# Adaptive-norm weights accumulated for pairs of feature blocks, and rotary tables made with the input tiles: one change to a decoder-layer kernel on one core

## The chip, the core and the metric

The kernel runs on one core of a Trainium2 chip. The metric is device time in microseconds (us) of one execution; before the change the median of three runs is 790.29 us (788.85 to 792.57). Inputs and output are float32 in HBM. The engines are named as in the profile: PE is the matmul engine (PEld its weight loads), DVE the vector engine, ACT the scalar engine, POOL GpSimd, SP the engine that issues nearly all DMAs.

## The reference, cut to what matters

One layer, 1024 tokens, 1024 features. The part that the change touches is the first: an adaptive norm, followed by the input projection.

```python
mod = jax.nn.silu(c) @ ada_w[l] + ada_b[l]          # (1, 1024) @ (1024, 3072)
shift, scl, gate = jnp.split(mod, 3, axis=-1)
h = rms_norm(x, norm_g[l]) * (1.0 + scl[:, None, :]) + shift[:, None, :]
proj = h @ w_in[l]                                  # split into 13 parts
...
ang = pos.astype(jnp.float32)[..., None] * inv      # rotary: cos(ang), sin(ang)
```

After it come two groups of attention heads, their gates, the output projection, a residual and a last norm. None of that is changed.

## The kernel before

**The stage.** `h` is needed with features on partitions, so `x` (8 tiles of 128 tokens) is scaled by its row norm, turned on PE (`xT`) and stored as `xnT`, 8 blocks of 128 features by 1024 tokens. Block k becomes `h` by one multiply and add per feature: `ab[:, 0, k]` (from `scl`) and `ab[:, 1, k]` (from `shift`) are one column each. ACT writes `hh[k]` (rounded to the matmul type) and `hf` (full float32), one after the other (`h_high`, L307 to L310); DVE makes `hl[k] = hf - hh[k]` (`h_low`, L312). Two parts of the projection are then accumulated over the eight blocks: `kcT` (`mm_kc`, 512-column products: four for hh with the weights' high part `whia`, four with their low part `wloa`, four for hl) and `ks` (`mm_ks`, 256 columns, as many). The low parts of the weights are made by POOL (`w_split`, L263) from DMA'd pieces that hold two blocks each.

**The modulation columns.** The weights for block k are 8 pieces (one per 128 inputs of `c`) of 128 x (2 x 128), loaded by `ad_load` as two tiles `ad` with four DMAs. In `mod_acc` the pieces 0 to 5 go to DVE: one `TENSOR_SCALAR` and five `SCALAR_TENSOR_TENSOR` of 256 columns build up `acc` (L288, L290). Pieces 6 and 7 go to PE as four one-column products (L284). `mod_mm` sums `acc` over partitions by two products with a column of ones (L297), and `mod_cols` makes the columns of `ab` in three small DVE instructions (L302 to L305). Block 0 is done by 16 one-column products on PE alone, spread over the last input tiles.

**The order.** The whole stage is inside one `manual_schedule` over all five engines, so each engine's order is that of the Python calls. First a loop over the input tiles (L463), whose step s has `x_stat(s)` (squares on ACT, `rv` on DVE), `x_turn(s - 1)` and `x_put(s - 2)`; `ACC0` adds parts of `mod_acc`. Then a software pipeline (L490) whose step s_ works on several blocks at once: weights for block s_ and s_ - 1 accumulated piece by piece between each other (`skew`), columns and `h_high` of block s_ - 1, and on PE the products with hh of block s_ - 2 and those with hl of block s_ - 3. The rotary tables are DVE work on 384 columns (`trig`, L394): their positions are loaded late (L459) and turned on PE in steps 3 to 5, and the tables stand in steps 7 and 8. The SP queue is in order: a load whose buffer is still in use holds the ones behind it. `x` and `ad` share 8 buffers of the tag `big`.

Of the kernel before, what the change touches and what calls it, by code (L numbers as in the profile page):

```python
# [107 lines left out]
def hybrid_block(ctx, tc, x, c, positions, ada_w, ada_b, norm_g, w_in, cmp_pos, cmp_k_w1, cmp_k_w2,  # L108
# [157 lines left out]
    def ad_load(k):  # L266
        ads[k] = []
        for q in range(AD_CUT):
            n = KD // AD_CUT
            ad = sp.tile([P, 1024], F32, name=f"ad{k}_{q}", tag="big", bufs=8).rearrange("p (k j n) -> p k j n", k=n, j=2)  # L270
# [21 lines left out]
    def mod_mm(k):  # L292
        if k in MOD_PE:
            return
        acc = accs.pop(k)
        for j in range(2):
            nc.tensor.matmul(pas[k][:, j:j + 1], acc[:, j, :], ones_pp[:, 0:1], start=False, stop=True,  # L297
                             skip_group_check=True)

    def mod_cols(k):  # L300
        pa = pas.pop(k)
        nc.vector.scalar_tensor_tensor(sums[:, k:k + 1], pa[:, 0:1], 1.0, cols[:, 16 + k:17 + k],  # L302
                                       op0=ALU.add, op1=ALU.add)
        nc.vector.tensor_tensor(ab[:, 0, k:k + 1], sums[:, k:k + 1], cols[:, 32 + k:33 + k], op=ALU.mult)
        nc.vector.tensor_tensor(ab[:, 1, k:k + 1], pa[:, 1:2], cols[:, 8 + k:9 + k], op=ALU.add)  # L305
# [141 lines left out]
    with tc.manual_schedule(engines={mybir.EngineType[e] for e in ENGS0}):  # L447
        nc.sync.dma_start(rows[0:8], c.rearrange("o (k p) -> (o k) p", p=P))
        x_load(0)
        small_loads()  # L450
        for t in range(1, X_AD):
# [7 lines left out]
        pos_loads()  # L459
# [3 lines left out]
        for s_ in range(NT + 2):  # L463
# [14 lines left out]
        def skew(k, i0, i1):  # L478
            for i in range(i0, i1):
                if k < KD:  # L480
                    mod_acc(k, 4 + i, 5 + i)
                if k + 1 < KD:
                    mod_acc(k + 1, i, i + 1)

# [4 lines left out]
        mod_acc(1, 2, 4)  # L489
        for s_ in range(1, KD + 3):  # L490
            if s_ + 1 < KD:
                ad_load(s_ + 1)
            if s_ % 2 == 1 and s_ // 2 + 1 < KD // 2:
                kc_raw(s_ // 2 + 1)
                ks_raw(s_ // 2 + 1)
            if 1 < s_ < KD:
                (kc_split if s_ % 2 else ks_split)(s_ // 2)
            if MOD_FIRST <= s_ <= KD:
                mod_mm(s_ - 1)
# [1096 lines left out]
```

## Time and profile before

| what | value |
|---|---|
| median of 3 runs | 790.29 us (788.85 to 792.57) |
| the profiled execution | 788.64 us, span 786.9 us |
| PE busy | 739.3 us, 94% of the span |
| DVE, ACT, POOL busy | 583.6, 396.3, 228.0 us |
| mean granted PE clock | 0.970 of full |
| the stage that the change touches | span start to about 82 us |

The profile is of one execution. Its time beside its span leaves 1.7 us that lie outside the first and last instruction. Times in the rows further below count from the span's start; busy shares are averages over stages with different limits, so what a change in the first 82 us is worth is read from those 82 us. A clock of 1.00 is PE's upper level (2.4 GHz), 0.50 the lower (1.2 GHz). A float32 product shows as two PE records, so four one-column products are "x8".

### The profile page before, as it was taken

To read this page: it belongs to the slowest core of one execution; us is meant where nothing else is said; L and a number is where in the kernel's file an instruction comes from. 1 tells how busy PE (TensorE), PEld (TensorE's weight loads), DVE (VectorE), ACT (ScalarE), POOL (GpSimd) and SP (SyncE) were. 2 spreads that over 40 slices of the span, in tenths; PEclk is the share of its full clock that TensorE was granted. 3 is DMA by queue.
4 is the path that set the end of the run, shared out by engine and by line. 5 is a ranking of instruction groups with operands and counts; after the bars stand their busy time and mean duration, and the time that the engine had idled before them with its cause. 6 is when DMAs were issued, how large, how long until landed. Compare 5 with 4: busy or idle time off the path is not lost.

```text
span 786.9 us, 17257 instructions
## 1 busy us (share of the span) xinstructions
PE 739.3 (94%) x6464; PEld 653.9 (83%) x6464; DVE 583.6 (74%) x1549; ACT 396.3 (50%) x697; POOL 228.0 (29%) x287
## 2 busy tenths in 40 slices
PE   4999999999999999997899999999988989999996
PEld 3988998989999999995677887777877777888885
DVE  3688745587688788888898889987888878654433
ACT  5354534133122331217899977987556566632212
POOL 3334433154231143504443312110200040154322
PEclk9599999999999999999999999999999979999999
DMA  8961423242531121103311123013010140435431
GB/s 307 262 197 49 127 55 108 61 121 80 162 95 48 44 52 47 36 31 97 93 47 44 43 56 82 22 57 80 10 28 16 52 151 29 151 131 185 144 113 54
DMA packets 60513, 70.18 MB, mean 89 GB/s; under 512 B 5957, under 2 KB 46728, under 8 KB 60430
## 3 DMA queue, kind: packets, MB, share of 16 engines
q1 hardware_dynamic: 55646, 64.62, 27.8%
q10 hardware_dynamic: 4784, 4.47, 1.7%
q8 instruction: 51, 0.84, 0.4%
q14 instruction: 32, 0.26, 0.1%
HBM read 48.33 MB, written 11.53 MB: 76 GB/s over the span
## 4 chain that ended last, share of the span: by engine, by line
PE 76%; DVE 9%; issue 4%; ACT 4%; DMA 4%; POOL 2%; SPq 1%; POOLq 0%; DVEq 0%; ACTq 0%
PE pj L589 24%; PE out L1528 11%; PE o L937 5%; PE pm L841 4%; PE s L994 3%; PE s L995 3%; PE kcT L321 2%; PE mo L937 2%; PE hid L642 2%; PE kq L1180 2%; PE ms L1301 2%; DVE L L1010 2%; PE ms L1302 2%; PE ms L1303 2%; PE mm L1256 2%
## 5 line engine op out<-in xcount | busy, mean ns | idle before, releaser
L589 PE MATMUL pj<-whi,hh 128*128 128x288 f32 (+2 forms) x544 | 161.4, 297 | 0.0
L589 PE MATMUL pj<-wlo,hh 128*128 128x288 f32 (+2 forms) x544 | 158.6, 292 | 0.0
L589 PE MATMUL pj<-whi,hl 128*128 128x288 f32 (+2 forms) x544 | 157.6, 290 | 0.0
L589 PEld LDWEIGHTS pj<-wlo,hh 128*128 128x128 f32 x544 | 102.5, 189 | 1.4
L589 PEld LDWEIGHTS pj<-whi,hh 128*128 128x128 f32 x544 | 102.5, 189 | 0.4
L589 PEld LDWEIGHTS pj<-whi,hl 128*128 128x128 f32 x544 | 102.2, 188 | 0.0
L1010 DVE TENSOR_TENSOR L<-E,H 128x1024 f16<-128x1024 f32 x74 | 92.0, 1243 | 13.1 <-ACT H L1005 11.4
L799 DVE CUSTOM_DVE_ANT_0 junk<-pm,maskw 128x256 bf16<-128x256 f32 (+3 forms) x160 | 77.7, 486 | 16.4 <-PE pm L841 4.4
L1004 ACT ACTIVATE E<-s 128x1024 f32<-128x1024 f32 x74 | 76.4, 1032 | 19.8 <-PE s L995 12.2
L937 PEld LDWEIGHTS <-H 128*128 128x128 f16 x1184 | 57.2, 97 | 30.2 <-issue 17.5
L968 POOL TENSOR_TENSOR mixn<-mixn,tmp 128x256 f32<-128x256 f32 x32 | 44.8, 1400 | 108.7 <-DVE tmp L967 101.9
L1005 ACT ACTIVATE H<-s 128x1024 f16<-128x1024 f32 x74 | 76.2, 1030 | 0.0
L841 PE MATMUL pm<-ka,qall 128*128 128x448 f32 (+5 forms) x208 | 67.2, 323 | 0.2 <-DVE mp L796 0.2
L937 PE MATMUL o<-v,H 128*128 128x65 f16 (+1 forms) x1056 | 60.0, 195 | 4.6 <-DVE mixn L964 4.6
L211 POOL TENSOR_TENSOR wlo<-wraw,whi 128x288 fp32r<-128x288 f32 (+2 forms) x64 | 51.7, 832 | 31.6 <-ACT whi L210 29.3
L994 PE MATMUL s<-qa,ka 128*128 128x512 f32 x132 | 57.9, 439 | 2.9 <-ACT H L1005 2.5
L937 PE MATMUL o<-v,L 128*128 128x65 f16 x528 | 56.7, 193 | 0.0
L937 PEld LDWEIGHTS <-L 128*128 128x128 f16 x592 | 55.7, 100 | 0.0
L708 ACT ACTIVATE zt<-pj 128x288 f32<-128x288 f32 (+1 forms) x32 | 12.2, 384 | 74.3 <-PE pj L589 62.6
L1314 ACT ACTIVATE lat<-ms 128x1024 f32<-128x1024 f32 (+2 forms) x40 | 32.6, 815 | 31.1 <-PE ms L1303 14.9
L1316 DVE TENSOR_TENSOR mL<-lat,mH 128x1024 f16<-128x1024 f32 (+2 forms) x40 | 39.0, 988 | 9.7 <-ACT mH L1315 9.5
L995 PE MATMUL s<-qall,kb_early 128*128 128x512 f32 x108 | 43.4, 401 | 0.0
(384 smaller groups left out, 1892.1 us busy)
## 6 DMA issues: line engine op xcount, KB each, us to landing
ad<-in_ada_w_dram SPq DMA_DIRECT2D x32, 256.0 KB
wraw<-in_w_in_dram SPq DMA_DIRECT2D x20, 288.0 KB
x<-in_x_dram SPq DMA_DIRECT2D x8, 512.0 KB
gw<-in_ada_w_dram SPq DMA_DIRECT2D x32, 128.0 KB
qa<-qall SPq DMA_DIRECT2D x32, 128.0 KB
wor<-in_w_out_dram SPq DMA_DIRECT2D x16, 256.0 KB
xr<-in_x_dram SPq DMA_DIRECT2D x8, 512.0 KB
out_dram<-y SPq DMA_DIRECT2D x7, 512.0 KB
```

The lines of the kernel that those rows point to most:

```text
L211: split.tensor_tensor(wlo[:, :width], raw[:, j, :width], f32(whi[:, :width]), op=ALU.subtract)
L589: nc.tensor.matmul(pt[:, :width], a[k][:, ts], b[:, :width], start=(n == 0), stop=(n == 23))
L799: nc.vector.tensor_tensor_reduce(out=junk[:, :w], in0=scores, in1=mask, scale=1.0, scalar=2.0 * NEG, op0=ALU.add, op1=ALU.max, accum_out=dst)
L841: nc.tensor.matmul(bank[:, :total_w], lhs, keys, start=True, stop=True)
L937: nc.tensor.matmul(po[:, c0:c0 + hi - lo], a[:n, qs], v[:, lo:hi], start=start and j == 0, stop=stop and j == 2, skip_group_check=True)
L968: nc.gpsimd.tensor_tensor(mv, mv, tmp, op=ALU.add)
L994: nc.tensor.matmul(dst, a, staged[u], start=True, stop=False)
L995: nc.tensor.matmul(dst, b, qc[u], start=False, stop=mk is None)
L1004: nc.scalar.activation(Et, pS, AF.Exp, scale=SC_NSA)
L1005: nc.scalar.activation(ph, pS, AF.Exp, scale=SC_NSA)
L1010: nc.vector.tensor_tensor(pl, Et, ph, op=ALU.subtract)
L1528: nc.tensor.matmul(po, a[:, kk], b[hf][k][:, cs.start - hf * 512:cs.stop - hf * 512], start=(n == 0), stop=(n == 23))
```

## The change

- **Pairs.** The blocks are handled in five groups, `GROUPS = ((0,), (1, 2), (3, 4), (5, 6), (7,))`. For a pair one `acc` of 512 columns holds both blocks (2 x 256), and all eight pieces go to DVE: one `TENSOR_SCALAR` and seven `SCALAR_TENSOR_TENSOR` of 512 columns for each of groups 1 to 3. Their one-column products on PE (pieces 6 and 7) are gone. Group 4 (block 7) keeps the form of before: six pieces of 256 columns on DVE, two on PE. The sum by ones is four products for a pair, the three column instructions work on two columns.
- **Loads.** `ad` pieces of a pair are runs of 256 columns; a pair has four tiles and eight DMAs, as two blocks had before.
- **Order.** The software pipeline is replaced by a loop over the groups. For a group: first pieces of the next group's `acc`, this group's columns, then for each block `h_high`, weight split, more pieces of the next `acc`, `h_low`, products with hh, products with hl. The sum by ones of the next group stands on PE just ahead of the last `ks` products of this group.
- **Tables.** The three position loads (L240 to L243 of before) are issued ahead of x tile 1; the turn of the positions and the table steps stand in the input loop (`TABS`), the last three steps after its last tile.

```diff
-AD_CUT = 2
-MOD_CUT = 1
-MOD_PE = (0,)
-MOD_DVE = 6
-MOD_FIRST = 4
-TAB0 = 4
+GROUPS = ((0,), (1, 2), (3, 4), (5, 6), (7,))
+MOD_DVE = (0, 8, 8, 8, 6)
+TABS = {6: 1, 7: 2, 8: 2, 9: 3}
...
+    def mod_acc(g, k0, k1):
+        w, first = len(GROUPS[g]) * P, MOD_DVE[g]
         if k0 == 0:
-            pas[k] = mx_bank(f"mod{k}")
+            pas[g] = mx_bank(f"mod{g}")
...
             if kk >= first:
                 for j in range(2):
-                    nc.tensor.matmul(pas[k][:, j:j + 1], src[:, j], sc[:, kk:kk + 1], start=(kk == first and j == 0),
+                    nc.tensor.matmul(pas[g][:, j:j + 1], src[:, j], sc[:, kk:kk + 1], start=(kk == first and j == 0),
...
             elif kk == 0:
-                accs[k] = sp.tile([P, 2, P], F32, name=f"acc{k}", tag="acc", bufs=2)
-                nc.vector.tensor_scalar(accs[k], src, sc[:, 0:1], None, op0=ALU.mult)
+                accs[g] = sp.tile([P, 512], F32, name=f"acc{g}", tag="acc", bufs=2)[:, :2 * w].rearrange("p (j n) -> p j n", j=2)
+                nc.vector.tensor_scalar(accs[g], src, sc[:, 0:1], None, op0=ALU.mult)
             else:
-                nc.vector.scalar_tensor_tensor(accs[k], src, sc[:, kk:kk + 1], accs[k], op0=ALU.mult, op1=ALU.add)
+                nc.vector.scalar_tensor_tensor(accs[g], src, sc[:, kk:kk + 1], accs[g], op0=ALU.mult, op1=ALU.add)
...
         small_loads()
+        pos_loads()
         for t in range(1, X_AD):
...
-        pos_loads()
...
+            if 3 <= s_ < 6:
+                next(post)
+            tables(TABS.get(s_, 0))
...
-        mod_acc(1, 2, 4)
-        for s_ in range(1, KD + 3):
...
+        for i in (1, 2, 3):
+            kc_raw(i)
+            ks_raw(i)
+            ad_load(i + 1)
+        mod_acc(1, 2, 5)
+        tables(9)
+        for g, blocks in enumerate(GROUPS):
+            after = g + 1 if g + 1 < len(GROUPS) else None
+            if g:
+                if after:
+                    mod_acc(after, 0, 2)
+                mod_cols(g)
+            for n, k in enumerate(blocks):
+                if g:
+                    h_high(k)
+                    if n == 0 and g < 4:
+                        kc_split(g)
+                        ks_split(g)
+                if after:
+                    mod_acc(after, *((5, 8) if n == len(blocks) - 1 else (2, 5)))
+                h_low(k)
+                mm_kc(k, (0, 1))
+                mm_ks(k, (0, 1))
+                mm_kc(k, (2,))
+                if after and n == len(blocks) - 1:
+                    mod_mm(after)
+                mm_ks(k, (2,))
```

The order of the instructions shows three places. The first is DVE at the end of the input tiles, before the change (`sums` and `ab` of `mod_278` are the columns of block 0, `acc_355` is block 1):

```order
L372 COPY xnT<-xT_1_341 128x4x128
L288 TENSOR_SCALAR acc_355<-ad_0_172,sc 128x256
L290 SCALAR_TENSOR_TENSOR acc_355<-ad_0_172,sc,acc_355 128x256
L302 SCALAR_TENSOR_TENSOR sums<-mod_278,cols 128x1
L304 TENSOR_TENSOR ab<-sums,cols 128x1
L305 TENSOR_TENSOR ab<-mod_278,cols 128x1
```

and DVE at the same place with the change (`acc_378` is the pair of blocks 1 and 2; `ang`, `cang` and those with a c are the tables):

```order
L371 COPY xnT<-xT_1_360 128x4x128
L286 TENSOR_SCALAR acc_378<-ad_0_175,sc 128x512
L288 SCALAR_TENSOR_TENSOR acc_378<-ad_0_175,sc,acc_378 128x512
L404 TENSOR_SCALAR ang<-ang 128x384
L404 TENSOR_SCALAR angc<-angc 64x32
L406 SCALAR_TENSOR_TENSOR cang<-ang 128x384
L406 SCALAR_TENSOR_TENSOR cangc<-angc 64x32
L409 TENSOR_SCALAR cang<-cang 128x384
L409 TENSOR_SCALAR cangc<-cangc 64x32
L301 SCALAR_TENSOR_TENSOR sums<-mod_288,cols 128x1
L303 TENSOR_TENSOR ab<-sums,cols 128x1
L304 TENSOR_TENSOR ab<-mod_288,cols 128x1
```

Between the last copy of `xnT` and the columns of block 0 stood two instructions; now two twice as wide and six of the tables stand there. What follows on DVE with the change (`hl_98` is block 0, `acc_485` the pair 3 and 4):

```order
L288 SCALAR_TENSOR_TENSOR acc_378<-ad_1_178,sc,acc_378 128x512 x2
L288 SCALAR_TENSOR_TENSOR acc_378<-ad_2_181,sc,acc_378 128x512 x2
L288 SCALAR_TENSOR_TENSOR acc_378<-ad_3_184,sc,acc_378 128x512 x2
L312 TENSOR_TENSOR hl_98<-hf_0_396,hh_90 128x1024
L286 TENSOR_SCALAR acc_485<-ad_0_411,sc 128x512
```

Six wide instructions stand ahead of the first `hl`, where eight of 256 columns (four of block 1, four of block 2) stood before.

The second is PE at the step from one group to the next with the change (`mod_484` is the sum of the pair 3 and 4, `hl_100` belongs to block 2, `hh_93` to block 3):

```order
L320 MATMUL kcT_1_390<-hl_100,whia 128x512
L296 MATMUL mod_484<-ones_pp,acc_485 128x1 x4
L328 MATMUL ks_0_391<-whi,hl_100 128x256 x2
L328 MATMUL ks_1_392<-whi,hl_100 128x256 x2
L320 MATMUL kcT_0_387<-hh_93,whia 128x512
```

and before, where `mod_426` is the sum of block 3, and the products behind it are those of block 2:

```order
L321 MATMUL kcT_1_361<-hl_98,whia 128x512
L329 MATMUL ks_0_362<-whi,hl_98 128x256 x2
L329 MATMUL ks_1_363<-whi,hl_98 128x256 x2
L297 MATMUL mod_426<-ones_pp,acc_427 128x1 x2
L321 MATMUL kcT_0_358<-hh_92,whia 128x512
```

Before, all 16 products with hh of block 2 and all 8 with hl of block 1 stood between the sum of block 3 and the first product with block 3's hh; now only four `ks` products stand between the sum of a pair and the first product with its hh.

The third is SP's queue of loads with the change:

```order
L233 DMA rows<-in_q_norm_g_dram 2x128
L234 DMA rows<-in_kv_norm_g_dram 1x128
L237 DMA pos_i<-in_positions_dram 8x128
L238 DMA posc_i<-in_positions_dram 63x1
L240 DMA inv<-in_freqs_dram 128x48
L346 DMA x_151<-in_x_dram 128x1024
```

The three position loads stood behind all tiles of x and the first `ad` of block 1; now tile 1 of x (`x_151`) and all that follows stand behind them.

## Rows read from the trace of the kernel before

**Rows 1.** The page, part 1: busy time and share of the span.

```profile
PE 739.3 (94%) x6464; PEld 653.9 (83%) x6464; DVE 583.6 (74%) x1549; ACT 396.3 (50%) x697; POOL 228.0 (29%) x287
```

**Rows 2.** Windows: stretch, busy us (x instructions) by engine, granted clock, DMA share, GB/s.

```profile
32.00:34.00 2.00, 1.86 (x9) 1.77 (x10) 1.89 (x7) 1.51 (x2) 0.00 (x0) 0.50 1.09 325
...
42.00:42.50 0.50, 0.50 (x3) 0.35 (x2) 0.18 (x1) 0.50 (x3) 0.00 (x0) 0.50 1.08 318
42.50:43.00 0.50, 0.50 (x3) 0.45 (x2) 0.50 (x1) 0.40 (x2) 0.34 (x1) 0.83 1.14 344
```

**Rows 3.** The chain that ended last, in order of time: start us, us, what.

```profile
32.49 1.25 ACT hh L310
...
33.78 3.78 PE kcT L321 x8
...
39.91 1.92 PE ks L329 x8
...
45.52 1.25 ACT hh L310
46.76 1.14 ACT hf L310
...
68.17 0.79 PE mod L284 x8
...
71.41 0.34 PE mod L297 x4
71.75 1.96 PE kcT L321 x8
73.71 0.95 PE ks L329 x8
74.66 0.93 PE kcT L321 x4
75.59 0.47 PE ks L329 x4
...
81.68 7.98 PE pj L589 x67
```

**Rows 4.** Timeline of DVE: start us, us, line, operation, count, idle before.

```profile
31.08 0.34 DVE L288 TENSOR_SCALAR acc<-ad,sc 128x256 f32<-128x256 f32 x1
...
31.97 0.16 DVE L302 SCALAR_TENSOR_TENSOR sums<-mod,cols 128x1 f32<-128x1 f32 x1
...
42.31 1.23 DVE L313 TENSOR_TENSOR hl<-hf,hh 128x1024 fp32r<-128x1024 f32 x1 [0.61 <-ACT hf L310]
43.46 0.96 DVE L290 SCALAR_TENSOR_TENSOR acc<-ad,sc,acc 128x256 f32<-128x256 f32 x1
...
45.40 1.91 DVE L290 SCALAR_TENSOR_TENSOR acc<-ad,sc,acc 128x256 f32<-128x256 f32 x4
...
74.03 0.36 DVE L405 TENSOR_SCALAR ang<-ang 128x384 f32<-128x384 f32 x1
...
75.29 0.17 DVE L410 TENSOR_SCALAR cangc<-cangc 64x32 f32<-64x32 f32 x1
```

**Rows 5.** Timeline of the SP queue: issue of DMAs.

```profile
20.23 0.30 SPq L241 DMA_DIRECT2D posc_i<-in_positions_dram  x1
20.58 0.36 SPq L243 DMA_DIRECT2D inv<-in_freqs_dram  x1
```

**Rows 6.** Timeline of ACT.

```profile
14.98 1.06 ACT L351 ACTIVATE sq<-x 128x1024 bf16<-128x1024 f32 x1 [1.82 <-DMA x<-in_x_dram]
```

**Rows 7.** Groups by form, DVE, first 82 us: busy us, mean ns of one.

```profile
L402 DVE SCALAR_TENSOR_TENSOR ang<-cang,ang 128x384 f32<-128x384 f32 x3 | 1.7, 555 | 0.0
...
L402 DVE SCALAR_TENSOR_TENSOR angc<-cangc,angc 64x32 f32<-64x32 f32 x3 | 0.5, 177 | 0.0
```

**Rows 8.** Timeline of POOL.

```profile
20.69 1.41 POOL L263 TENSOR_TENSOR wloa<-wrawa,whia 128x256 fp32r<-128x256 f32 x2
...
42.66 2.34 POOL L263 TENSOR_TENSOR wloa<-wrawa,whia 128x256 fp32r<-128x256 f32 x2 [3.27 <-ACT whia L262]
```

More of the change, by code (lines that the diff above doesn't have):

```diff
@@ L264, in w_split, with ad_load @@
             dst[2 * k2 + j] = (whi, wlo)
[L266 to L270, printed above, removed]
-            for j, o in ((0, D), (1, 0)):
-                nc.sync.dma_start(ad[:, :, j, :], ada_r[:, q * n:(q + 1) * n, o + k * P:o + (k + 1) * P])
-            ads[k].append(ad)
-    def mod_acc(k, k0, k1):
+    def ad_load(g):
+        ads[g] = []
+        w = len(GROUPS[g]) * P
+        n = 512 // w
+        for q in range(KD // n):
+            ad = sp.tile([P, 1024], F32, name=f"ad{g}_{q}", tag="big", bufs=8).rearrange("p (k j n) -> p k j n", k=n, j=2)
+            for j, o in ((0, D), (1, 0)):
+                c0 = o + GROUPS[g][0] * P
+                nc.sync.dma_start(ad[:, :, j, :], ada_r[:, q * n:(q + 1) * n, c0:c0 + w])
+            ads[g] += [ad[:, i] for i in range(n)]
@@ L294, in mod_mm @@
+                nc.vector.tensor_scalar(accs[g], src, sc[:, 0:1], None, op0=ALU.mult)
+            else:
+                nc.vector.scalar_tensor_tensor(accs[g], src, sc[:, kk:kk + 1], accs[g], op0=ALU.mult, op1=ALU.add)
+    def mod_mm(g):
+        if MOD_DVE[g] == 0:
             return
-        acc = accs.pop(k)
+        acc, m = accs.pop(g), len(GROUPS[g])
         for j in range(2):
-            nc.tensor.matmul(pas[k][:, j:j + 1], acc[:, j, :], ones_pp[:, 0:1], start=False, stop=True,
-                             skip_group_check=True)
@@ L300, in mod_cols @@
-    def mod_cols(k):
-        pa = pas.pop(k)
-        nc.vector.scalar_tensor_tensor(sums[:, k:k + 1], pa[:, 0:1], 1.0, cols[:, 16 + k:17 + k],
+            for i in range(m):
+                nc.tensor.matmul(pas[g][:, j * m + i:j * m + i + 1], acc[:, j, i * P:(i + 1) * P], ones_pp[:, 0:1],
+                                 start=(MOD_DVE[g] == KD and j == 0 and i == 0), stop=True, skip_group_check=True)
+    def mod_cols(g):
+        pa, k, m = pas.pop(g), GROUPS[g][0], len(GROUPS[g])
+        nc.vector.scalar_tensor_tensor(sums[:, k:k + m], pa[:, 0:m], 1.0, cols[:, 16 + k:16 + k + m],
@@ L303, in mod_cols @@
                                        op0=ALU.add, op1=ALU.add)
-        nc.vector.tensor_tensor(ab[:, 0, k:k + 1], sums[:, k:k + 1], cols[:, 32 + k:33 + k], op=ALU.mult)
-        nc.vector.tensor_tensor(ab[:, 1, k:k + 1], pa[:, 1:2], cols[:, 8 + k:9 + k], op=ALU.add)
+        nc.vector.tensor_tensor(ab[:, 0, k:k + m], sums[:, k:k + m], cols[:, 32 + k:32 + k + m], op=ALU.mult)
+        nc.vector.tensor_tensor(ab[:, 1, k:k + m], pa[:, m:2 * m], cols[:, 8 + k:8 + k + m], op=ALU.add)
     def h_high(k):
@@ L477, in hybrid_block @@
         pks = [o_bank(f"ks0_{i}", i) for i in range(2)]
[L478 to L483, printed above, removed]
         mod_mm(0)
@@ L488, in hybrid_block @@
         ks_split(0)
-        mod_acc(1, 2, 4)
-        for s_ in range(1, KD + 3):
[L491 to L499, printed above, removed]
-            if 0 <= s_ - 2 < KD:
-                mm_kc(s_ - 2, (0, 1))
-            skew(s_, 0, MOD_CUT)
-            if 1 < s_ <= KD:
-                if s_ < MOD_FIRST:
-                    mod_mm(s_ - 1)
-                mod_cols(s_ - 1)
-                h_high(s_ - 1)
-            skew(s_, MOD_CUT, 4)
-            if 2 < s_ < 6:
-                next(post)
-            if s_ == KD - 1:
-                tables(TAB0)
-            if s_ == KD:
-                tables(9)
-            if s_ - 1 < KD:
-                h_low(s_ - 1)
-            if 0 <= s_ - 2 < KD - 1:
-                mm_ks(s_ - 2, (0, 1))
-            if 0 <= s_ - 3 < KD:
-                mm_kc(s_ - 3, (2,))
-                if s_ - 3 == KD - 1:
-                    mm_ks(s_ - 3, (0, 1))
-                mm_ks(s_ - 3, (2,))
+        for i in (1, 2, 3):
[25 more added lines that the diff above has]
+                mm_ks(k, (2,))
         start.close()
```

6 lines of the change are left out of this document (1 added, 5 removed).

## The prediction

> **What bounds the kernel now.** I read the page first: PE is busy 94% of the span [rows 1], so over most of the kernel a delay of PE's queue goes into the end one for one. The reader should then go to the stage that is changed, up to 82 us, and ask what sets its pace; the average does not say it. The windows show the granted clock: 0.50 while the input tiles are turned and block 0 starts, and full again about 42.7 us [rows 2]. The chain of waits shows the beats: hh of block 0 starts at 32.49, its first products at 33.78, the next stage's `pj` at 81.68 [rows 3]. Inside, one block at the upper clock costs PE 1.96 + 0.95 + 0.93 + 0.47 = 4.31 us of real products, 0.79 for four one-column products and 0.34 for the sum by ones, 5.4 in all [rows 3]. The beat is 5.6: hh and hf on ACT, 1.25 + 1.14, then `hl` on DVE, 1.23, which had waited 0.61 for hf, then DVE's accumulations and columns before ACT may start again [rows 3, 4]. So two loops have nearly the same length, PE's 5.4 and that through ACT and DVE. Work taken from PE alone gains little; what matters is the length of the DVE loop and what stands in front of it.
>
> **Part 1, position loads.** Two of the three took 0.30 and 0.36 us of SP's queue and start 0.35 apart [rows 5]; I take the third like them: three cost 1.1 us, ahead of tile 1 of x and of all loads behind it. ACT waited 1.82 us for the x tile whose squares start at 14.98 [rows 6], so that stage runs on loads, and a late queue makes late tiles; from there PE turns tiles without a pause, and the delay stays. I take +1.1. Lower bound 0, if the loads in flight hide it.
>
> **Part 2, in front of the columns of block 0.** From 31.08, where the last copy of `xnT` lets go of DVE, to `sums` at 31.97 stand two 256-column instructions, 0.89 us [rows 4]. Now they have 512 columns, and six table instructions follow. Those six took 75.46 - 74.03 = 1.43 us where they stood [rows 4]. For the width: 384 columns took 555 ns, 32 took 177 [rows 7], which is 1.07 ns per added column; 256 columns in a run of four took 1.91 / 4 = 0.48 us [rows 4], so 512 take 0.48 + 0.27 = 0.75 (an estimate); the `TENSOR_SCALAR`, 0.34 now [rows 4], I put at 0.45. Together 2.63, that is +1.75. The table steps that move into the earlier steps of the input loop, and the turn of the positions on PE, I cost at nothing: DVE has pauses between tiles there, since PE turns them at the lower clock. Were that cover gone, their six `SCALAR_TENSOR_TENSOR` would cost 3 x (0.555 + 0.177) = 2.2 us [rows 7], and the other steps less than that. hh of block 0 starts at 32.49 + 1.1 + 1.75 = 35.3.
>
> **Part 3, group 0.** Behind the columns DVE has six `SCALAR_TENSOR_TENSOR`, 6 x 0.75 = 4.5, then `hl` 1.2. POOL makes two low parts meanwhile. Such a pair took 1.41 us when DVE paused and 2.34 beside DVE [rows 8], and a 256-column instruction beside it took 0.96 instead of 0.48 [rows 4]: I charge DVE 0.45 for each POOL instruction. That is 4.5 + 0.9 + 1.2 = 6.6. PE has 1.3 for hh, then 3.78 + 1.92 at the lower clock [rows 3], 7.0 in all. Then four `kcT` products with hl, 0.93, eight records of the sum by ones, 0.68, 0.1 to get to DVE, and 0.5 from `sums` to hh (32.49 - 31.97): group 1 starts at 35.3 + 9.3 = 44.6. If PE is still at the lower clock there, it is 1.5 later.
>
> **Part 4, groups 1 and 2.** From a pair's first hh: hf after 2.4, with the first three wide instructions beside it; `hl` 1.2; three wide ones 2.25; four POOL instructions 1.8; `hl` 1.2. That is 8.85, and PE, 1.3 + 4.31 + 1.96 + 0.95 = 8.5, is ready just before. Then 0.93 + 0.68 + 0.1 + 0.5 = 2.2, since the sum stands behind the last `hl`, and the next hh waits for it: 11.0 per pair. Before, two blocks took 2 x 5.6 = 11.2. Here is where the saved products go: PE loses 24 of them, but behind each sum it waits 1.25 for hh plus 0.6 for the columns with only 0.47 of `ks` products to do. I had two ends here: without any cost of POOL 10.7 (PE's own sum), with DVE held for the whole of each POOL instruction 13.6.
>
> **Part 5, groups 3 and 4, and the sum.** DVE's next group is narrow (256 columns, six pieces), so PE sets the pace: 1.3 + 4.31 + 0.79 + 4.31 - 0.47 + 0.34 + 0.6 = 11.2; the last block 1.3 + 4.31 = 5.6. `pj` starts at 44.6 + 22.0 + 11.2 + 5.6 = 83.4, against 81.68: **1.7 us later**. Wider runs in the `ad` loads I cost at nothing: DVE does not wait for them in the loop. Behind the stage PE goes on, so the profiled execution's 788.64 becomes 790.3. The median of the runs shown is 1.65 above that execution; against it I forecast **792.0 us**. A measurement of this kernel can tell about 0.5% (3.95 us) from no change, so this is no change. With part 1 at 0 and part 4 at 10.7 it would be 790.3, with part 4 at 13.6 797.2.
>
> **A rule against the width.** The rows say that a `SCALAR_TENSOR_TENSOR` on float32 pays 1.07 ns per added column, beside a fixed part [rows 7]. In the Trainium skill, Vector Engine (DVE) Microarchitecture Reference, section 7, one point says that this instruction with two sources in SBUF that are not bf16 runs at half its throughput. By that an added column would cost twice the 1.07, a wide one 0.48 + 0.55 = 1.03 (an estimate from that point and these rows), and the forecast would be some 4 us higher. The 384-column row, at 0.555 beside 0.48 for 256 columns, speaks against it, and the sum goes by the rows.
>
> **The rivals.**
> - *Faster (chance 0.06): PE's time is given back whole.* If the DVE loop hid behind PE, the five quartets of blocks 2 to 6 would go from the path: one at the lower clock, about 1.7 (twice 0.79 and a little), and four at 0.79, that is 4.9, and parts 1 and 2 were hidden: 790.3 - 4.9 = 785.4. For it speaks PE's 94%, against it that `hl` waits for hf, and hf for the columns [rows 4].
> - *Even (0.12): the front is hidden.* Loads and tables cost nothing, and the groups gain 0.2 to 0.3 each: 789.5.
> - *Slower (0.11): POOL holds DVE.* If a wide instruction waits for the whole POOL instruction (1.17 instead of 0.45), ten of them beside the groups 0 to 2 cost 7 us, less 0.5 that PE hides: 798.5. It decides from about 0.8 us on for each. The pair at 42.66 to 45.00 speaks against it: both engines made progress.
> - *Slower (0.05): the clock comes back one group later.* At the lower clock a pair costs PE about 19.4 instead of 11.0 [rows 3]: 800.4. For it speaks that PE idles about 3 us at 32 to 35 us where it now has one-column products; against it that the products of group 0 then stand without one-column ones between them. The rule of the Trainium skill that fits is in TensorE: Matmul & The Clock Gate, Part 1: an engine left idle for long gets half its clock, and sustained work gives it back. No row of this stage shows a fall after the rise.
> - *Slower (0.04): no discount for width.* If twice the columns cost twice the 0.48, a wide one is 0.96: 13 of them stand on the path (1, 6, 3 and 3), +2.7, and the first three of groups 1 and 2 no longer fit beside hf, +0.9: 795.6. That is how the rule of section 7 above would act; the 384-column row has it at 0.555, where this would be 0.72.
>
> **How the numbers follow.** My forecast has the rest, 0.62, from 789.5 to 794.5 (part 1 from 0 to 1.1, the lower clock in group 0, and the 1.8 us by which medians move). Faster by over 0.5% (below 786.3): most of the first rival, 0.05. Slower (above 794.2): the three slow rivals nearly whole, 0.19, and 0.01 of the forecast, 0.20. The range goes from 787.5 to 797.0: outside lie the fast rival, most of the POOL one and the clock.
>
> **What would show it.** Right: wide instructions at 0.75 us alone; `sums` of block 0 near 34.8, hh at 35.3; a wait of PE for hh of 1.2 to 1.5 us at each of the groups 1 to 4; pairs 10.7 to 11.3 us apart; `pj` near 83.4, and the rest of the span as long as before. Wrong: tile 4 of x landing no later, pairs at 10 or 13 us, the clock's rise far from 40 to 44 us, or a difference that arises behind `pj`.

## The result, and the profile after the change

| | before | with the change |
|---|---|---|
| median | 789.4 us (784.6 to 793.2, 14 runs) | 796.41 us (792.22 to 798.7, 14 runs) |
| profiled execution | 788.64 us, span 786.9 | 797.98 us, span 796.2 |
| `hh` of block 0 | 32.49 us | 35.23 us |
| first `pj` on PE | 81.52 us | 87.20 us |
| `hh` of block 0 to `pj` ("the loop") | 49.03 us | 51.97 us |

The ratio is 1.0079, 95% interval 1.0055 to 1.0103: slower, by 6 us by the ratio and 7.0 by the medians. (`pj` is read from PE's timeline here. The chain in [rows 3] has 81.68 for it, which the prediction used; the 0.16 changes nothing.)

The page's busy line, beside [rows 1], gives no hint of a loss: PE and its weight loads do less, DVE as much as before.

```profile
PE 735.9 (92%) x6416; PEld 648.8 (81%) x6416; DVE 584.4 (73%) x1528; ACT 396.1 (50%) x697; POOL 230.6 (29%) x287
```

The beats do. The timeline of ACT (start us, us, what, idle time before and what ended it) has `hh` of the first block of each group; before, block 0 stood at 32.49 [rows 3]:

```profile
35.23 1.24 ACT L309 ACTIVATE hh<-xnT,ab 128x1024 fp32r<-128x1024 f32 x1 [3.89 <-DVE ab L304]
...
44.10 1.24 ACT L309 ACTIVATE hh<-xnT,ab 128x1024 fp32r<-128x1024 f32 x1 [5.89 <-DVE ab L304]
...
55.40 1.24 ACT L309 ACTIVATE hh<-xnT,ab 128x1024 fp32r<-128x1024 f32 x1 [5.42 <-DVE ab L304]
...
67.74 1.24 ACT L309 ACTIVATE hh<-xnT,ab 128x1024 fp32r<-128x1024 f32 x1 [6.47 <-DVE ab L304]
...
79.23 1.24 ACT L309 ACTIVATE hh<-xnT,ab 128x1024 fp32r<-128x1024 f32 x1 [1.40 <-DVE ab L304]
```

The groups take 8.87, 11.30, 12.34 and 11.49 us, the last block 7.97 to `pj`. Groups 1 and 2 run the same code and differ by 1.04. PE's timeline shows a wait for `hh` of about 1.2 us at each step, and one that the prediction did not have, for the copies `lat`, ahead of `pj`:

```profile
45.40 1.20 PE L320 MATMUL kcT<-hh,whia 128*128 128x512 f32 x4 [1.21 <-ACT hh L309]
...
56.69 1.53 PE L320 MATMUL kcT<-hh,whia 128*128 128x512 f32 x4 [1.22 <-ACT hh L309]
...
69.03 1.20 PE L320 MATMUL kcT<-hh,whia 128*128 128x512 f32 x4 [1.21 <-ACT hh L309]
...
80.52 1.48 PE L320 MATMUL kcT<-hh,whia 128*128 128x512 f32 x4 [1.48 <-ACT hh L309]
...
87.20 0.38 PE L576 MATMUL pj<-whi,hh 128*128 128x256 f32 x1 [0.67 <-ACT lat L443]
```

Four `kcT` products took 1.20 behind two of these waits, 1.53 and 1.48 behind the others. The windows (columns as in [rows 2]; the granted clock stands third from the end) say why: PE was put back to half its clock behind the second and the fourth wait.

```profile
56.00:57.00 1.00, 0.31 (x1) 0.30 (x2) 0.93 (x3) 1.00 (x2) 0.00 (x0) 1.00 1.12 329
57.00:58.00 1.00, 1.00 (x4) 0.75 (x3) 0.79 (x2) 1.00 (x3) 0.00 (x0) 0.69 0.70 214
58.00:60.00 2.00, 2.00 (x7) 1.61 (x6) 2.00 (x2) 2.00 (x5) 1.85 (x2) 0.50 0.01 2
...
81.00:82.00 1.00, 1.00 (x5) 0.77 (x4) 0.36 (x1) 0.60 (x1) 0.00 (x0) 0.63 0.80 255
82.00:84.00 2.00, 2.00 (x8) 1.62 (x7) 0.86 (x1) 0.00 (x0) 0.00 (x0) 0.50 0.36 106
```

Before the change nothing of the kind followed the rise at 42.7 [rows 2]; the windows from there to `pj`, before:

```profile
43.00:60.00 17.00, 16.23 (x105) 14.31 (x104) 15.01 (x34) 9.22 (x14) 7.18 (x7) 1.00 0.57 167
60.00:81.50 21.50, 21.50 (x135) 19.18 (x134) 18.27 (x44) 9.65 (x15) 7.67 (x9) 1.00 0.29 82
```

DVE's timeline has the wide accumulations at the price the prediction gave them: three took 2.32 us alone, and three beside POOL 3.52, with `hl` at 1.76 instead of 1.23.

```profile
43.98 2.32 DVE L288 SCALAR_TENSOR_TENSOR acc<-ad,sc,acc 128x512 f32<-128x512 f32 x3
46.51 1.23 DVE L312 TENSOR_TENSOR hl<-hf,hh 128x1024 fp32r<-128x1024 f32 x1 [0.21 <-ACT hf L309]
47.65 3.52 DVE L288 SCALAR_TENSOR_TENSOR acc<-ad,sc,acc 128x512 f32<-128x512 f32 x3
51.10 1.76 DVE L312 TENSOR_TENSOR hl<-hf,hh 128x1024 fp32r<-128x1024 f32 x1
```

Behind `pj` the profiled execution of before took 705.4 us (786.9 - 81.52), that of the change 709.0. I don't count the 3.6 between them as the change's: over the fourteen profiles of this study this stretch, whose code is the same in all, took 705.1 to 711.0, without order.

### The profile page after: what moved, and what is told of

Its sections match the earlier page's. It is cut to its first block, busy times and chain, and to the rows that moved or that the text cites. A ratio compares the mean times of both kernels' runs of the same rounds, so it can differ in the third digit from the quotient of the medians.

```text
span 796.2 us, 17138 instructions
## 1 busy us (share of the span) xinstructions
PE 735.9 (92%) x6416; PEld 648.8 (81%) x6416; DVE 584.4 (73%) x1528; ACT 396.1 (50%) x697; POOL 230.6 (29%) x287
## 4 chain that ended last, share of the span: by engine, by line
PE 71%; DVE 9%; issue 8%; DMA 5%; ACT 3%; POOL 2%; SPq 1%; POOLq 0%; DVEq 0%; ACTq 0%
PE pj L576 21%; PE out L1515 11%; PE o L924 5%; PE s L981 3%; PE pm L828 3%; PE s L982 3%; PE mo L924 2%; PE kcT L320 2%; PE ms L1288 2%; PE hid L629 2%; PE kq L1167 2%; PE ms L1289 2%; PE ms L1290 2%; PE mm L1243 2%; PE qr L1212 1%
## 5 line engine op out<-in xcount | busy, mean ns | idle before, releaser
L786 DVE CUSTOM_DVE_ANT_0 junk<-pm,maskw 128x256 bf16<-128x256 f32 (+3 forms) x160 | 77.8, 486 | 16.1 <-PE pm L828 4.2
```

The costliest lines, as they stand in the source:

```text
L786: nc.vector.tensor_tensor_reduce(out=junk[:, :w], in0=scores, in1=mask, scale=1.0, scalar=2.0 * NEG, op0=ALU.add, op1=ALU.max, accum_out=dst)
```

## The experiments

Theory: the loss is made in the first 87 us, by a later front (loads and tables) and by PE's waits at the group steps, which cost their own length and now and then the clock. Rivals: the queue alone delays the front; VectorE sets the pairs; the falls have another cause. All runs, in the order of the text; "front" is `hh` of block 0, "falls" counts the steps into groups 1 to 4 behind which the granted clock fell. Front, loop, `pj` and falls are read from one profiled execution each; a ratio is to runs of the kernel before taken beside that version's, whose medians were 789.4 to 791.15, so it need not be the quotient of two medians of the table:

| kernel | front | loop | `pj` | falls | median us | ratio to before (95%) |
|---|---|---|---|---|---|---|
| before | 32.49 | 49.03 | 81.52 | 0 | 789.4 | |
| the change | 35.23 | 51.97 | 87.20 | 2 | 796.41 | 1.0079 (1.0055 to 1.0103) |
| loads on ACT's queue | 32.35 | 52.08 | 84.43 | 2 | 797.56 | 1.0102 (1.0062 to 1.0142) |
| last tables late | 34.18 | 50.21 | 84.39 | 1 | 794.6 | 1.0058 (1.0029 to 1.0088) |
| pairs only | 32.48 | 53.39 | 85.87 | 2 | 795.88 | 1.0062 (1.0036 to 1.0087) |
| front only | 32.18 | 47.96 | 80.14 | 0 | 791.9 | 1.0040 (1.0010 to 1.0071) |
| sum early | 35.63 | 47.40 | 83.03 | 0 | 790.62 | 1.0012 (0.9982 to 1.0041) |
| fill, sums' bank | 35.97 | 59.90 | 95.87 | 4 | 800.78 | 1.0154 (1.0112 to 1.0196) |
| fill, spare bank | 33.48 | 49.41 | 82.89 | 0 | 794.25 | 1.0050 (1.0027 to 1.0073) |
| last block's order | 35.27 | 50.08 | 85.35 | 1 | 794.25 | 1.0058 (1.0029 to 1.0087) |
| all mends | 29.28 | 47.45 | 76.73 | 0 | 789.97 | 0.9998 (0.9963 to 1.0034) |
| all mends, front filled | 29.11 | 47.66 | 76.77 | 0 | 786.06 | 0.9959 (0.9931 to 0.9987) |
| before, front filled | 28.41 | 50.16 | 78.57 | 0 | 788.01 | 0.9987 (0.9954 to 1.0019) |
| all mends, filled more | 28.18 | 46.77 | 74.95 | 0 | 787.01 | 0.9963 (0.9933 to 0.9992) |

By these intervals, medians of two versions that lie some 2 us apart can't be told from each other. Clearly apart from the change are the sum early, the fill in the sums' bank, the versions with all mends and the kernel before with its front filled.

**How to read "front".** It has three parts, which the traces show one by one: up to the end of the last x tile's squares on ACT (how late the tiles land), from there to the last copy of `xnT` on DVE, and from that copy to `sums`; `hh` follows `sums` by 0.50 to 0.52 in all. ACT's and DVE's timelines have them, first before,

```profile
21.75 0.19 ACT L351 ACTIVATION_READ_ACCUMULATOR sq<-x 128x1 f32 x1
...
30.47 0.69 DVE L372 COPY xnT<-xT 128x512 f32<-128x512 f32 x1 [2.62 <-PE xT L362]
```

then with the change,

```profile
22.88 0.19 ACT L350 ACTIVATION_READ_ACCUMULATOR sq<-x 128x1 f32 x1
...
31.60 0.69 DVE L371 COPY xnT<-xT 128x512 f32<-128x512 f32 x1 [1.47 <-PE xT L361]
...
34.73 0.14 DVE L301 SCALAR_TENSOR_TENSOR sums<-mod,cols 128x1 f32<-128x1 f32 x1
```

and so for the others:

| kernel | last squares | to last copy | copy to `sums` | clock fell at |
|---|---|---|---|---|
| before | 21.75 | 8.72 | 1.50 | 18.8 |
| the change | 22.88 | 8.72 | 3.13 | 19.8 |
| last tables late | 23.16 | 8.72 | 1.79 | 18.9 |
| pairs only | 21.47 | 8.72 | 1.79 | 18.5 |
| front only | 22.43 | 6.52 | 2.73 | 26.0 |
| loads on ACT's queue | 22.20 | 6.52 | 3.13 | 25.9 |
| fill, spare bank | 22.64 | 7.21 | 3.13 | 24.1 |
| all mends | 22.01 | 4.98 | 1.78 | 25.3 |

The change's 2.74 is 1.13 from the tiles and 1.63 behind the last copy. The middle part holds a clock effect. In the eleven profiles without a filled front the clock fell between 17.6 and 19.8 us (seven of them) or between 24.1 and 26.0 (four), not by the kernel. In all seven the middle part took 8.72 or 8.73, with the early table steps and without them; in the four it was 1.5 to 3.7 shorter. So the first and the last part are compared by themselves, the loop by itself, and fronts only at early falls.

**Position loads on ACT's queue.**

```diff
-        nc.sync.dma_start(pos_i, positions.rearrange("o (k p) -> (o k) p", p=P))
+        nc.scalar.dma_start(pos_i, positions.rearrange("o (k p) -> (o k) p", p=P))
...
-        nc.sync.dma_start(inv, bass.AP(tensor=freqs.tensor, offset=freqs.offset, ap=[[0, P], [1, NINV]]))
+        nc.scalar.dma_start(inv, bass.AP(tensor=freqs.tensor, offset=freqs.offset, ap=[[0, P], [1, NINV]]))
```

> The three position loads go from SP's queue to ACT's, which is idle there until tile 0 of x lands; all else as in the change. Theory (SP's queue makes the x tiles late, forecast +1.1 us): the squares of tile 4 start near 15.0 us instead of 16.07, hh of block 0 near 34.1 instead of 35.23, pj 1.1 us earlier. Rival (the loads are limited by what the DMA engines move, and the position loads hide in that): squares of tile 4 still at 16, hh at 35.2, no gain.

The squares of tile 4 started at 15.80, with the change at 16.07, before at 14.98 [rows 6]. SP's queue no longer had the three loads, and got little back: the issue of three x tiles took 2.19 us there, 1.29 with the change.

```profile
3.40 2.19 SPq L346 DMA_DIRECT2D x<-in_x_dram  x3
```

So it is not the place in SP's queue. That the small loads in flight hold up the tiles fits, but the later runs weaken it: with the loads late, tile 4's squares stood at 14.98, 14.70, 15.61, 16.17, 15.87 and 15.25, with them early (eight profiles) at 15.80 to 16.42. The means, 15.4 and 16.1, leave 0.7 us, less than the late ones differ among themselves. The median did not fall. (The front at 32.35 is a late fall, at 25.9.)

**The last three table steps in group 3.**

```diff
-TABS = {6: 1, 7: 2, 8: 2, 9: 3}
+TABS = {6: 1, 7: 2, 8: 2}
...
-        tables(9)
...
+                if g == 3 and n == 0:
+                    tables(9)
```

> The last three table steps (1.43 us of DVE) go from between the last input tile and the columns of block 0 to group 3, where DVE waits for hf; all else as in the change. Theory: sums of block 0 at 33.4 instead of 34.73 and hh at 33.85 instead of 35.23; group 3 no longer than 11.5 us, since PE paces it; pj 1.4 us earlier. Rival (PE's last one-column products and not DVE hold the columns): sums stay at 34.7; or the steps make hl of block 5 late and group 3 grows by 0.4 or more.

From the last copy of `xnT` to `sums` it now took 1.79 instead of 3.13:

```profile
31.88 0.69 DVE L371 COPY xnT<-xT 128x512 f32<-128x512 f32 x1 [1.46 <-PE xT L361]
...
33.67 0.15 DVE L301 SCALAR_TENSOR_TENSOR sums<-mod,cols 128x1 f32<-128x1 f32 x1
```

That is 1.34, near the 1.43 that DVE's rows gave these steps [rows 4]. The front is only 1.05 earlier (34.18), as the last tile came 0.28 later. `pj` is 2.8 earlier, and one of the change's two falls did not come. Group 3, where PE sets the pace, took 11.30 us with them (11.49 without).

**The pairs alone, and the front alone.** One has loads and tables where they stood, with the accumulations by pairs; the other is the kernel before with only the early loads and tables. The first against the change:

```diff
         small_loads()
-        pos_loads()
...
+        pos_loads()
...
-            tables(TABS.get(s_, 0))
...
-        tables(9)
...
+                if g == 3 and n == 0:
+                    tables(1)
...
+                if g == 3:
+                    tables((2, 9)[n])
```

and the second against the kernel before:

```diff
         small_loads()
+        pos_loads()
...
-        pos_loads()
...
+            if 3 <= s_ < 6:
+                next(post)
+            tables({6: 1, 7: 2, 8: 2, 9: 3}.get(s_, 0))
...
-            if s_ == KD - 1:
-                tables(TAB0)
-            if s_ == KD:
-                tables(9)
```

> The pair scheme alone: position loads and tables stand where they stood before the change, the accumulations by pairs stay. Theory (the front of block 0 pays for the loads and for the early table steps, and nothing gives it back): squares of tile 4 near 15.0 us as before the change (16.07 with it), hh of block 0 at about 32.9 (35.23), total about 2.4 us under the changed kernel. Rival (the group loop absorbs a later start): group 0 is longer by what the front wins, pj within 0.5 us of the changed kernel's 87.2, total within 1 us of its 796.4.

> The kernel before with only the early position loads and the early tables; one-column products and the old accumulations stay. Theory: squares of tile 4 near 16.1 us, hh of block 0 near 35 (32.49), pj near 84 (81.5), total about 2.5 us over the kernel before. Rival (the tables leave VectorE's later groups, and the group loop wins back what the front loses): pj within 0.5 us of 81.5, total within 1 us of the kernel before.

Pairs only starts at 32.48, like before, but not for the same reasons. DVE's timeline:

```profile
30.19 0.69 DVE L370 COPY xnT<-xT 128x512 f32<-128x512 f32 x1 [2.61 <-PE xT L360]
...
31.98 0.15 DVE L300 SCALAR_TENSOR_TENSOR sums<-mod,cols 128x1 f32<-128x1 f32 x1
```

From the last copy to `sums` it took 1.79, before 1.50: the two wide instructions cost 0.29, and a last tile that came 0.28 earlier hid it. Of the 2.75 us by which it is ahead of the change, 1.41 is the tiles and 1.34 the last tables. But only 0.5 us of the median came back, for the tables now stand in group 3 (13.86 us, with a fall, instead of 11.49): the theory's total was wrong, and the rival's, which was right, came another way than it said, for group 0 is as long as with the change (8.93 against 8.87). What is left, 53.39 - 49.03 = 4.4 us in the loop, is the pairs' own loss. Front only was expected near 35 and had 32.18, with the fall at 26.0: its tiles came 0.68 later than before and its last tables took 1.23, but the late fall made the middle part 2.2 shorter. It wins 1.07 back in the loop, where the tables are gone. By the ratio it is 3.2 us above before (0.8 to 5.6 by the interval). Both parts lose; neither needs the other.

**The sum ahead of the products with `hl`, the columns ahead of the next pieces.**

```diff
             if g:
+                mod_cols(g)
                 if after:
                     mod_acc(after, 0, 2)
-                mod_cols(g)
...
                 mm_ks(k, (0, 1))
-                mm_kc(k, (2,))
                 if after and n == len(blocks) - 1:
                     mod_mm(after)
+                mm_kc(k, (2,))
                 mm_ks(k, (2,))
```

> The sum by ones of the next group stands ahead of the last block's products with hl instead of behind the four kcT ones, and the columns ahead of the next but one group's first pieces; all else as in the change. Theory (the chain hl, kcT products, sum, columns, hh makes PE wait 1.2 us and more at each group, and these waits bring the clock down): group 1 starts 1.6 us after hl's start less, groups 1 and 2 take 10.3 us each instead of 11.3 and 12.3, group 3 10.5 instead of 11.5, no wait of PE for hh over 0.6, no stretch at the lower clock after 41 us, pj at 80 to 83 us instead of 87.2, total some 5 us shorter. Rival (DVE's work sets the length of a pair, the place of the sum does not matter): pairs stay at 11 us and pj within 1.5 us of 87.

PE now has four `kcT` products more to do while the columns and `hh` are made, and its wait at the step shrinks from 1.22 to 0.29. But the pair still took 11.55 us, since four wide accumulations now stand ahead of the first `hl` (3.65 us beside POOL), and PE waits for that. PE's timeline of group 2:

```profile
48.58 1.20 PE L320 MATMUL kcT<-hl,whia 128*128 128x512 f32 x4 [1.40 <-DVE hl L312]
...
55.64 1.20 PE L320 MATMUL kcT<-hh,whia 128*128 128x512 f32 x4 [0.29 <-ACT hh L309]
```

The wait moved rather than went, and the expected 10.3 us was missed. Still the loop is 4.6 us shorter than the change's and 1.6 shorter than that of before: no fall came, group 0 took 7.17, and the median is 5.8 us under the change.

**Filling the wait.** Four dummy products of 448 columns behind the last `ks` products of a group: first into the bank of the sums themselves (`pas[after]`), in columns nobody uses, then into the bank of the sums whose columns have already been read (`spare[0]`).

```diff
                 mm_ks(k, (2,))
+                if after and n == len(blocks) - 1:
+                    for _ in range(4):
+                        nc.tensor.matmul(pas[after][:, 8:456], hh[k][:, :P], hh[k][:, :448], start=False, stop=True, skip_group_check=True)
```

> At each step from one group to the next PE gets four 448-column products whose results nobody reads (into unused columns of the bank of the sums), behind the last ks products, where it waits for hh; all else as in the change. Theory (the two stretches at the lower clock, 57.3 to 60.7 and 81.1 to 84.6 us, come from PE's waits at the group steps): the granted clock stays at 1.00 from 41 us to pj, group 2 takes 11.1 us instead of 12.3, the last block 1.5 us less, pj near 84.2, total some 3 us shorter though PE has more to do. Rival (the falls come from something else): they come as often, pj at 87 or later.

> The changed kernel with four dummy products of 448 columns behind the sums of each group, into the bank of the previous group's sums, which nothing reads any more: TensorE has work in its wait for hh, and nothing waits for that work. Theory (the clock falls because of TensorE's waits at the group steps): granted clock 1.00 from its rise near 41 us to pj, group 2 near 11.2 us (12.34), last block 1.5 us shorter (7.97), pj near 84.3 (87.20), total about 3 us under 796.4. Rival (the falls have another cause): they come as often as without the fill, pj near 87, total near 796.

The first missed its aim. The columns read that bank, so they waited for the filler, PE's wait behind the filler was 1.79 at every step, and the clock fell behind all four. PE's timeline and the windows at the first:

```profile
47.53 1.40 PE L320 MATMUL kcT<-hh,whia 128*128 128x512 f32 x4 [1.79 <-ACT hh L309]
```

```profile
46.00:48.00 2.00, 0.47 (x2) 0.43 (x3) 1.93 (x5) 1.76 (x2) 0.00 (x0) 1.00 1.01 346
48.00:49.00 1.00, 1.00 (x5) 0.81 (x4) 0.79 (x2) 1.00 (x3) 0.00 (x1) 0.68 1.00 351
49.00:51.00 2.00, 2.00 (x7) 1.61 (x7) 2.00 (x2) 2.00 (x5) 2.00 (x2) 0.50 0.13 47
```

The second does what was meant. PE's timeline at the step into group 2, and the windows from the rise on:

```profile
53.57 0.97 PE L516 MATMUL mod<-hh 128*128 128x448 f32 x4
54.94 1.20 PE L323 MATMUL kcT<-hh,whia 128*128 128x512 f32 x4 [0.40 <-ACT hh L312]
```

```profile
38.00:50.00 12.00, 10.91 (x64) 9.20 (x63) 10.68 (x15) 5.87 (x8) 5.02 (x5) 1.00 0.68 218
50.00:60.00 10.00, 9.37 (x56) 7.91 (x56) 8.69 (x13) 5.87 (x8) 3.62 (x4) 1.00 0.47 135
60.00:70.00 10.00, 9.37 (x54) 7.87 (x53) 7.00 (x12) 5.07 (x8) 3.63 (x4) 1.00 0.10 29
70.00:80.00 10.00, 9.32 (x57) 7.96 (x56) 3.49 (x5) 4.59 (x7) 5.63 (x8) 1.00 0.41 111
80.00:82.80 2.80, 2.23 (x16) 1.85 (x14) 1.73 (x5) 0.72 (x2) 0.00 (x0) 1.00 0.52 151
```

`hh` comes at the same distance as before the edit (group 1 is 11.30 in both), only PE is not idle. Group 2 takes 11.28 (12.34), the last block 6.43 (7.97), the loop 2.56 less. That is the price of two falls, by itself. The median is 2.2 lower, which is not clear of noise (1.0050, with 1.0027 to 1.0073, against 1.0055 to 1.0103): work that is of no use made this stage shorter; whether it made the kernel shorter is not shown. Nor is one profile without a fall much by itself, since without filler 12 of 20 such steps had none either (last section).

**The last block's order.** `kcT` with `hl` ahead of all `ks` products, in the last block only.

```diff
                 mm_kc(k, (0, 1))
+                if k == KD - 1:
+                    mm_kc(k, (2,))
                 mm_ks(k, (0, 1))
...
-                mm_kc(k, (2,))
+                if k < KD - 1:
+                    mm_kc(k, (2,))
```

> The changed kernel with the last block's four kcT products of hl put back ahead of all its ks products, as before the change. Theory (pj waits for lat because the last kcT product stands only four ks products ahead of it): pj waits under 0.1 us for lat (0.67), hh of the last block to pj shorter by 0.7 us, and nothing else moves; total 0.7 us under 796.4, less than the timing can tell. Rival (the copies of lat are late for another reason): pj waits as long.

The wait for `lat` is gone: the copies start at 84.40 and `pj` follows the last `ks` product at once.

```profile
82.90 1.19 PE L320 MATMUL kcT<-hl,whia 128*128 128x512 f32 x4 [0.26 <-DVE hl L312]
...
85.35 0.28 PE L579 MATMUL pj<-whi,hh 128*128 128x256 f32 x1
```

The last block took 6.13, against 6.43 where the clock held too (fill in the spare bank): 0.3 of the 0.7, since PE meets `hl` 0.26 too early. The median is 2.2 lower, which is not clear of noise, and this profile has one fall less than the change's.

**All mends.** Tables and loads late, the sum and the columns early, three pieces of the next `acc` ahead of the first `hl` and five behind, piece 7 of each later pair on PE, the last block's order.

```diff
...
-MOD_DVE = (0, 8, 8, 8, 6)
+MOD_DVE = (0, 7, 7, 7, 6)
...
-                    mod_acc(after, *((5, 8) if n == len(blocks) - 1 else (2, 5)))
+                    mod_acc(after, *((5 if g == 0 else 3, 8) if n == len(blocks) - 1 else (2, 3)))
...
```

> All of the mends at once: positions and tables late as before the change, the sum ahead of the two accumulations of hl, the columns ahead of the next pieces, the last piece of each later group back on TensorE, the last block's kcT products ahead of its ks products. Theory: hh of block 0 near 32.9 us, groups of 10.3 to 11 us, no wait of TensorE for hh over 0.7 us, no fall of the clock after its rise, no wait of pj for lat, pj at 78 to 80, total 1 to 3 us under the kernel before (789.4). Rival (VectorE's order sets the group, as in the run with the sum early): groups of 11.5 us or more, pj at 81 to 82, total as before the change.

Pairs took 10.75 us, waits for `hh` were 0.42 at most, no fall followed the rise at 35.5, `pj` waited for nothing. `pj` at 76.73 is flattered by a fall of the front at 25.3. With the front of pairs only, 32.48 with the fall at 18.5, it would be about 80 (an estimate: 32.48 + 47.45). Against before that is 1.6 us, the difference of the loops. The median shows no difference (interval 0.9963 to 1.0034). So the scheme, put right, can't be told from the kernel before.

**Filling the front.** Forty dummy transposes of the identity into an unused bank, in PE's idle stretches: 20 ahead of the first transpose, 13 behind it, 7 behind the third tile. In the version with all mends, and in the kernel before; then 87 in the former (23, 36 and 17 at these places, and 11 in the wait for `hh` of block 0).

```diff
+        fl = o_bank("fill", 0)
+        def fill(n):
+            for _ in range(n):
+                nc.tensor.transpose(fl[:, :P], ident, ident)
+        fill(20)
         pr = mx_bank("rowsT")
...
+        fill(13)
         for s_ in range(NT + 2):
...
+            if s_ == 3:
+                fill(7)
```

> The version with all mends (789.97 us, clock falls at 25.6 us in its profile) with 40 dummy transposes of the identity into an unused bank in TensorE's idle stretches of the front: 20 ahead of the rows' transpose, 13 behind it, 7 behind the third tile. Theory (the clock's fall in the front answers TensorE's idle time there, and it prices the front at about 0.5 us for each us at 0.50): granted clock 1.00 from the first tile to pj, hh of block 0 at 27 to 28.5 us (29.28 with the fall at 25.6, about 31.5 with a fall at 19), pj near 75, total 2 to 4 us under the version without them, 786 to 788. Rival (the front waits for transfers, or the fall comes anyway): hh of block 0 at 29 to 32, total 789 to 791; filler that stands ahead of the first tiles can also cost up to 1 us.

> The kernel before with the same 40 dummy transposes in the front. Theory: granted clock 1.00 through 20 to 43 us where it was 0.50, hh of block 0 at 28 to 29 us (32.49), kcT products of block 0 at 1.96 instead of 3.78, pj at 76 to 78 (81.5), total 3 to 5 us under the kernel before. Rival (the fall comes anyway, or the front waits for transfers): hh at 31 to 33, pj at 80 to 82, total as before.

> The filled version (786.06 us) with 87 dummy transposes instead of 40, so that the three waits it left are covered too: 23 ahead of the rows' transpose, 36 behind it (TensorE idled from 8.0 to 11.3 us there and the clock fell at 11.2), 17 behind the third tile (1.57 us left), 11 in the wait for hh of block 0 (1.95 us, the clock fell at 28). Theory (each fall answers the wait ahead of it): granted clock 1.00 from 10 us to pj, kcT products of block 0 at 1.2 for four instead of 2.08, group 0 shorter by 0.5 to 1 us, pj near 76 (76.8), total 0.5 to 1 us under 786.06. Rival (a fall comes with sustained work too): a fall between 10 and 40 us remains, pj 76.5 to 78, total 786 to 787.

The clock did not stay at 1.00 in the first two. Windows of the first: it fell at 11.7 behind an idle stretch that the fill had left open (8 to 11 us), rose near 15, and fell near 28.7 in the wait for `hh` of block 0.

```profile
8.00:11.00 3.00, 0.02 (x1) 0.00 (x0) 0.55 (x2) 1.60 (x4) 0.32 (x1) 1.00 1.03 350
...
12.00:15.00 3.00, 2.97 (x14) 2.49 (x14) 2.41 (x5) 2.23 (x4) 1.88 (x2) 0.50 1.08 353
...
16.00:28.00 12.00, 9.48 (x86) 9.01 (x83) 8.44 (x17) 8.12 (x16) 5.37 (x6) 1.00 0.98 336
...
29.00:35.00 6.00, 4.60 (x13) 3.86 (x14) 5.71 (x7) 2.98 (x4) 1.90 (x2) 0.50 1.04 350
```

But the fall that stood at 18 to 26 us without fill was later, and its cost smaller. The mended version went from 789.97 to 786.06 us, 0.9959 of before (0.9931 to 0.9987): the first version here that beats both kernels. The kernel before gained too little to tell (0.9987): its front came 4.1 us earlier, but group 0 ran at half clock up to 41.7, and the loop was 1.1 longer. With 87 dummies the first fall came at 29.4 and ended near 32.8, as the windows show,

```profile
11.00:28.00 17.00, 13.96 (x123) 13.01 (x121) 12.09 (x26) 10.20 (x20) 7.39 (x8) 1.00 0.99 339
...
29.00:32.00 3.00, 2.52 (x6) 2.05 (x7) 2.89 (x4) 2.17 (x4) 1.06 (x2) 0.57 1.06 356
```

and `pj` at 74.95. The median, 787.01, is the same within what can be told. The rival's fall remained.

## Why the prediction was right or wrong

The time lies in the range (787.5 to 797.0), 4.4 us above the forecast. But the interval of the ratio lies above 1.005, so the case that I gave 0.75, no change that can be told, is not the one that came; it is the one I gave 0.20. That 796.41 is still inside the range is in part luck: my forecast's own case ended at 794.5, and the range reached 797.0 for rivals that did not come.

**Parts 1 and 2, the front: right, in sum and in split.** Forecast 35.3, measured 35.23; `sums` at 34.73 (forecast 34.8). The last tile came 1.13 later (forecast 1.1). The wide instructions cost 0.29 (0.3) and the last three table steps 1.34 (1.43). The earlier steps cost nothing: from the last squares to the last copy it took 8.72 with them and without. What the runs do not bear out is the reason for the 1.1. The run with ACT's queue shows that the place in SP's queue is not it, and as the loads leave 0.7 at tile 4 over all profiles, part of the 1.13 is scatter.

**Part 3: right in sum.** 8.87 against 9.3 (its terms add up to 9.2). The clock rose at 40.3, so PE was done with `hh` before the 7.0 had passed, and DVE's `hl` came last: PE waited 0.32 for it.

**Part 4: the mechanism right, one assumption wrong.** Group 1 took 11.30 against 11.0. The prices held: 0.77 for a wide instruction (2.32 / 3), and 0.44 for each POOL instruction on DVE: 3.52 + 1.76 - 3 x 0.77 - 1.23 = 1.74 for four. The wait for `hh`, forecast 1.2 to 1.5, came at 1.21 to 1.48. The step that failed is the silent one: every product behind the rise was priced at the upper clock. I wrote that no row of this stage shows a fall after the rise, which was true of a trace whose PE never had such a wait there, and so had only a rival with a late rise. The waits I forecast are the ones behind which the clock fell, at two of four steps. Group 2 took 12.34. (With each POOL instruction at the 1.17 of the rival, the upper end comes to 13.9 by these terms, not 13.6; nothing rests on it.)

**Part 5: too short by 2.7.** Group 3 was 0.3 longer than forecast, the last block 2.4 (7.97 against 5.6): 1.54 is the second fall, 0.67 the wait of `pj` for `lat`, 0.2 the rest. I let `pj` follow the last block's products without asking who frees its banks. Before the change the last `kcT` product had twelve `ks` products behind it, with the change four, and the copies no longer fit behind them.

In sum `pj` is 3.8 later than forecast (87.20 against 83.4): the two falls 2.6, `lat` 0.7, the groups 0.5. That is nearly the miss in the median.

**The rivals.** POOL holds DVE for 0.44, not for its whole instruction, so that rival fell. Width has its discount (0.77, not 0.96). On both the rows were right. The rule of the Trainium skill (Vector Engine (DVE) Microarchitecture Reference, section 7), by which the prediction estimated 1.03 for a wide one, is not borne out: it took 0.77. PE's saved products were not given back, as they weren't on the path. What decided is that PE's clock fell behind waits of 1.2 to 1.5 us at some of the group steps. The rule of the Trainium skill in TensorE: Matmul & The Clock Gate, Part 1, by which idle PE loses its clock, I had used only for the late rise. The traces agree with it as far as no fall came at the steps whose wait was filled or shortened to 0.7 us or less; I had read it as a rule on long idleness, and here the measured waits decide.

## What to carry to other kernels

- When a change leaves the engine that bounds the kernel with a new wait, price the wait twice: its length, and a stretch at half clock that can follow it (here 1.06 and 1.54 us). That a trace has no fall says nothing for an order with other waits.
- If the wait can't be removed, give PE work in it into a bank that nobody reads, and make sure that nothing waits for the filler; into the spare bank the filler made this loop 2.6 us shorter, into the wrong bank the same filler made it 7.9 us longer.
- At the end of a stage ask which copies free the next stage's banks, and how many instructions stand behind the last product they read.

## What the runs showed of the hardware

- **Falls against waits.** Of PE's 20 waits for `hh` of 0.92 to 2.30 us at group steps (five profiles: the change, loads on ACT's queue, last tables late, pairs only, last block's order) eight were followed by a fall; of four of 1.79 us (fill in the sums' bank) all; of the 20 steps with 0.7 us or less (sum early, fill in the spare bank, all mends and its two filled versions) none. The length alone does not decide: with the sum early, PE waited 1.40 us for `hl` between long products, and no fall followed; and at 29.4 us, with 87 dummies, one came behind a wait of 0.79. What else counts is open.
- **The same code falls at different places.** Five profiles have the front of the change, line for line. Its clock fell at 17.6, 19.0, 19.8, 19.8 and 24.1 us, and the last fall made the middle part of the front 1.5 us shorter than the others. The all-mends version's twelve runs go from 782.88 us (mean granted clock 0.987) to 794.28 (0.963). A single profile can't rank versions that lie 3 us apart; the loop's length and the median could.
- **POOL beside DVE.** The two POOL pairs of group 1 ran beside the DVE rows of the section on the result:

```profile
46.86 2.62 POOL L260 TENSOR_TENSOR wloa<-wrawa,whia 128x256 fp32r<-128x256 f32 x2 [6.98 <-ACT whia L259]
49.44 2.33 POOL L260 TENSOR_TENSOR wlo<-wraw,whi 128x256 fp32r<-128x256 f32 x2
```

From the first `hl` at 46.51 to the end of the second at 52.86, three wide accumulations, two `hl` and these four POOL instructions took 6.35 us. One after the other they would be 3 x 0.77 + 2 x 1.23 + 4 x 0.70 (half of the free pair in [rows 8]) = 7.6, an estimate. So both engines went on, each slowed. The Trainium skill's SBUF — State Buffer, section "SBUF: two separate sides", has the port that both share locked for a whole instruction, which would give the 7.6; the trace does not agree.
